# A hybrid HGRN2 and short-convolution layer on one core: tokens split from PSUM, their sums made in the first pairs, squares made later, small steps moved between engines

## The chip, the cores and the metric

The kernel runs on one core of one Trainium2 chip. The metric is the device time of one execution in microseconds. TensorE is PE in the rows below, VectorE is DVE, ScalarE is ACT, GpSimd is POOL, and SyncE is SP.

## The reference

One inference step of one decoder layer. The tokens are 16 meta tokens, a prompt of 512 and 8 samples of 4 tokens, 560 in all, 2048 wide. Cut to what matters:

```python
hn = rmsnorm(h, pre_norm_w)
proj = hn @ w_in                                  # 2048 -> 8192
q, fz, i, za, bg, cg, xt, zb = split(proj)        # 8 parts of 1024
f = lb + (1 - lb) * sigmoid(fz)                   # lb from softmax, cumsum
k = (1 - lb) * sigmoid(-fz);  v = i
o, S = hgrn(q, k, log(max(f, 1e-30)), v)          # S_t = f_t S_{t-1} + k_t v_t, o_t = S_t q_t; 8 heads of 128
o = rmsnorm(o, hgrn_norm_w) * silu(za)
c, new_buf = short_conv(cg * xt, buf, conv_w)     # causal, width 3
yb = bg * c * silu(zb)
h = h + rmsnorm(concat(o, yb) @ w_out, post_norm_w)
```

The outputs are the layer's result for prompt and samples, the new recurrent states and the new convolution buffers.

## The kernel before

**Input projection.** `w_in` is worked through in 32 *pairs* `p` of two blocks of 128 output columns, four pairs to each of 8 heads: 4i holds the forget gate and the input i, 4i+1 holds q and the gate za (the gate pair), 4i+2 holds C and x~ (the conv pair), 4i+3 holds B and zb. A pair has four raw blocks of 512 KB, named 11, 12, 21, 22 (which half of the output, which half of the 2048), loaded two pairs ahead by SP's queue into six buffers.

To multiply float32 in float16, a block is scaled by a power of two and split in a high and a low half: `split_w` makes the high on ScalarE (L290) and the low on VectorE (L291). The power comes from the sum of squares of the pair: `squares` (L263, ScalarE, with an accumulator) and `scale_of_weights` (L265 on), where a product with ones (`pss`, L275) sums over the partitions and `power` (L239 to L241) makes the scale. A product of two split operands is 24 matmuls: 8 chunks of 128 by three lines, L353 to L355 in `product`.

**Seven or eight products.** A plain pair takes eight block products. A pair for which `seven(p)` holds takes seven, with sums of weight blocks s1 to s4 (`sum_w`, L300, VectorE) and sums of token blocks t1 to t4 (`t_steps`, L454 on). Its plan is 11, s1, s2, 12, s3, s4, 22. Three partial results, m1, t and q, are put into SBUF by ScalarE (L370) so that their PSUM tile can be used again: product 3 writes where product 1 wrote, and the `sink` calls add them back on VectorE (L372, L374). `PLAIN` is the first pair that may take seven; before, it is 2.

**Tokens.** `turn_x(hf, k)` transposes 280 tokens by 128 features into PSUM. ScalarE copies that with the norm's weight to a float32 tile (`big`), POOL casts two of them to float16 (the high half), VectorE makes the low half. The token sums t1 to t4 are made from the float32 tiles during pair 1: two of them on POOL, two on VectorE.

**Order.** `pair(p)` runs the products of pair p; ahead of each, `step(j)` calls one of the next pair's preparations (`prep_steps(p + 1)`). Blocks 11 and 21 of pair p+2 are squared at step 5, the other two at the next pair's step 0. The recurrence of a head, the generator `attend`, is advanced in small pieces between the products of the pairs that follow; its tiles carry the names pd, vbd, lv, kc, pss, dm, ds, po, zur. In it, the intra-chunk part casts `vbd` on ScalarE (L688) for the products `lv` (L692); `dm` (L822) and `ds` (L827) form the state, in two PSUM banks that `pss` uses too; the rmsnorm of the head's output squares it (L842), sums (L849, L851), makes 1/sqrt by three Newton steps on VectorE (L858 to L860) and scales (L861). Up to the first lines of the recurrence the program keeps the written order; from there on a scheduler places the instructions by its own estimates, each engine then running its queue in order.

**After the projection** comes the output projection with the post norm (L973 on), which is not touched.

Of the kernel before, what the change touches and what calls it, by code (L numbers as in the profile page):

```python
# [64 lines left out]
def hymba_kernel(  # L65
# [389 lines left out]
    def t_steps():  # L455

        b11, b21, b12_, b22 = (bf[:, hf, KC * j:KC * j + KC] for hf in range(2) for j in range(2))

        def do(n, dst, a, b, op, eng, sign, c):
            c = slice(4 * c, 4 * c + 4)  # L460
            d = dst[:, c].rearrange("p k t -> p (k t)")
            h, l = (t[:, c].rearrange("p k t -> p (k t)") for t in xop(n))
            eng.tensor_tensor(d, a[:, c].rearrange("p k t -> p (k t)"), b[:, c].rearrange("p k t -> p (k t)"), op=op)
            A.activation(h, d, AF.Copy, scale=sign)
            V.scalar_tensor_tensor(l, d, sign, h, op0=ALU.mult, op1=ALU.subtract)

        for args in (("t1", b11, b11, b12_, ALU.subtract, G, 1.0), ("t3", b12_, b22, b12_, ALU.subtract, G, 1.0),
                     ("t2", b22, b22, b11, ALU.add, V, -1.0), ("t4", b21, b22, b21, ALU.subtract, V, 1.0)):
            for c in range(2):
                yield lambda args=args, c=c: do(*args, c)  # L470
# [191 lines left out]
    def attend(h, f, kb, q, vt, g):  # L662
# [185 lines left out]
        A.activation(sq[0:NS, SEQ:640], po_s, AF.Square)  # L848
        V.tensor_reduce(ssq[:, 0:4], sq[:, 0:SEQ].rearrange("p (j v) -> p j v", v=P),  # L849
                        axis=mybir.AxisListType.X, op=ALU.add)  # L850
        V.tensor_reduce(ssq[0:NS, 4:5], sq[0:NS, SEQ:640], axis=mybir.AxisListType.X, op=ALU.add)  # L851
# [9 lines left out]
        V.tensor_tensor(  # L861
            sq[:, 0:SEQ].rearrange("p (j v) -> p j v", v=P), po.rearrange("p (j v) -> p j v", v=P),
            r[:, 0:4].rearrange("p (j o) -> p j o", o=1).to_broadcast([P, 4, P]), op=ALU.mult,
        )
# [383 lines left out]
```

## Time and profile before

| | us |
|---|---|
| median of 3 runs | 1094.87 (1093.39 to 1099.02) |
| profiled execution, its own time | 1097.03 |
| its span on the core | 1095.3 |
| TensorE busy | 1015.4, 93% |
| VectorE busy | 819.2, 75% |
| ScalarE busy | 596.3, 54% |
| POOL busy | 77.5, 7% |

The mean granted clock of TensorE in the profiled execution is 0.972 of full speed. In the rows of groups by line and shape stands: line, engine, operation, output <- inputs with partitions x elements and type, count; then busy us and mean ns of one; then the idle time ahead of them and what ended it. In a timeline row: start, duration, engine, line, operation, and in brackets the idle time ahead with its releaser.

### The profile page before, as it was taken

What the parts mean: (1) busy time and instruction counts of PE and PEld (TensorE: products, weight loads), DVE (VectorE), ACT (ScalarE), POOL (GpSimd) and SP (SyncE); (2) the same over time, 40 slices, a digit from 0 to 9 for tenths busy, and PEclk for the clock granted to TensorE, in tenths of its full rate; (3) what the DMA queues carried; (4) which work ended last, traced back from release to release, by engine and by line L of the source; (5) the groups of instructions that cost most, each with busy time, mean ns of one, the idle gap of its engine ahead of it and who ended that gap; (6) DMA issues with size and microseconds to landing.
All of it is one profiled execution on the core that took longest, in us unless ns stands there. A gap on an engine that the chain in (4) does not pass through costs nothing.

```text
span 1095.3 us, 20032 instructions
## 1 busy us (share of the span) xinstructions
PE 1015.4 (93%) x8099; PEld 855.9 (78%) x8099; DVE 819.2 (75%) x1765; ACT 596.3 (54%) x1032; POOL 77.5 (7%) x83
## 2 busy tenths in 40 slices
PE   4798999989999999999999999999999999999995
PEld 3455878778777877787787778777778899999995
DVE  6468889888888988899889989888889762223226
ACT  4457846674566567466745665674566253232323
POOL 1362000000000000000000000000000010000004
PEclk9968999999999999999999999999999999999998
DMA  9212313441343224224503432242244154222104
GB/s 306 58 39 77 115 41 96 120 135 34 87 122 109 66 85 124 78 79 127 145 22 98 129 103 77 76 121 77 78 119 153 42 210 141 99 85 99 57 1 164
DMA packets 156931, 109.33 MB, mean 100 GB/s; under 512 B 3729, under 2 KB 151362, under 8 KB 155766
## 3 DMA queue, kind: packets, MB, share of 16 engines
q1 hardware_dynamic: 152934, 92.90, 28.6%
q0 software_dynamic: 3680, 14.49, 4.4%
q8 instruction: 63, 1.03, 0.4%
q10 hardware_dynamic: 224, 0.66, 0.2%
q14 instruction: 30, 0.25, 0.1%
HBM read 98.79 MB, written 9.25 MB: 99 GB/s over the span
## 4 chain that ended last, share of the span: by engine, by line
PE 36%; DVE 25%; DMA 18%; ACT 12%; issue 4%; POOL 1%; DVEq 0%; ACTq 0%; SPq 0%
DMA raw<-in_w_in_dram 18%; DVE ws L291 7%; DVE w L291 5%; ACT junk L263 4%; ACT w L290 4%; PE omm L1055 3%; PE omm L1056 3%; PE omm L1054 3%; DVE s L300 3%; PE omm L1064 2%; PE omm L1063 2%; PE omm L1062 2%; PE mm L353 2%; PE mm L354 2%; PE mm L355 2%
## 5 line engine op out<-in xcount | busy, mean ns | idle before, releaser
L263 ACT ACTIVATE junk<-raw 128x1024 uint8<-128x1024 f32 x120 | 126.8, 1057 | 131.8 <-DMA raw<-in_w_in_dram 130.9
L353 PE MATMUL mm<-x_b,w 128*128 128x272 f16 (+1 forms) x592 | 167.7, 283 | 0.9 <-ACT f L370 0.9
L354 PE MATMUL mm<-x_b,w 128*128 128x272 f16 (+1 forms) x592 | 167.3, 283 | 0.0
L355 PE MATMUL mm<-x_b,w 128*128 128x272 f16 (+1 forms) x592 | 167.2, 283 | 0.0
L291 DVE SCALAR_TENSOR_TENSOR w<-raw,sc,w 128x1024 f16<-128x1024 f32 x102 | 130.1, 1279 | 31.8 <-ACT w L290 30.9
L353 PEld LDWEIGHTS <-w 128*128 128x128 f16 x1120 | 110.5, 99 | 24.1 <-issue 1.4
L354 PEld LDWEIGHTS <-w 128*128 128x128 f16 x1120 | 110.5, 99 | 23.8 <-issue 2.9
L290 ACT ACTIVATE w<-raw,sc 128x1024 f16<-128x1024 f32 x102 | 115.7, 1139 | 22.9 <-DVE sc L241 18.9
L355 PEld LDWEIGHTS <-w 128*128 128x128 f16 x1120 | 110.5, 99 | 21.9
L353 PE MATMUL ma<-x_t,ws 128*128 128x274 f16 (+2 forms) x352 | 101.9, 290 | 17.1 <-ACT e L370 17.1
L354 PE MATMUL ma<-x_t,ws 128*128 128x274 f16 (+2 forms) x352 | 101.7, 289 | 0.0
L355 PE MATMUL ma<-x_t,ws 128*128 128x274 f16 (+2 forms) x352 | 101.7, 289 | 0.0
L185 DVE TENSOR_TENSOR wl<-rawo,wh 128x1024 fp32r<-128x1024 f32 x32 | 39.2, 1224 | 80.0 <-ACT wh L184 80.0
L290 ACT ACTIVATE ws<-s,sc 128x1024 f16<-128x1024 f32 x66 | 75.2, 1139 | 39.1 <-DVE s L300 37.9
L354 PEld LDWEIGHTS <-ws 128*128 128x128 f16 x704 | 70.2, 100 | 30.6 <-issue 17.1
L291 DVE SCALAR_TENSOR_TENSOR ws<-s,sc,ws 128x1024 f16<-128x1024 f32 x66 | 84.3, 1277 | 8.9 <-ACT ws L290 6.4
L353 PEld LDWEIGHTS <-ws 128*128 128x128 f16 x704 | 70.0, 99 | 16.6 <-issue 2.5
L355 PEld LDWEIGHTS <-ws 128*128 128x128 f16 x704 | 70.2, 100 | 15.2
L184 ACT CAST wh<-rawo 128x1024 fp32r<-128x1024 f32 x32 | 33.6, 1051 | 79.8 <-PE omm L1063 70.4
L1054 PE MATMUL omm<-mh,wh 128*128 128x288 f32 x256 | 75.8, 297 | 0.0
L1055 PE MATMUL omm<-ml,wh 128*128 128x288 f32 x256 | 75.6, 295 | 0.0
L1056 PE MATMUL omm<-mh,wl 128*128 128x288 f32 x256 | 75.4, 295 | 0.0
(317 smaller groups left out, 2671.9 us busy)
## 6 DMA issues: line engine op xcount, KB each, us to landing
raw<-in_w_in_dram SPq DMA_DIRECT2D x128, 512.0 KB, 4.2
rawo<-in_w_out_dram SPq DMA_DIRECT2D x32, 512.0 KB, 3.4
xp<-in_x_prompt_dram SPq DMA_DIRECT2D x4, 1024.0 KB, 10.6
s<-in_state_hgrn_dram POOLq DMA_DIRECT2D x8, 512.0 KB, 4.9
out_dram<-s POOLq DMA_DIRECT2D x8, 512.0 KB, 3.9
xres<-in_x_prompt_dram POOLq DMA_DIRECT2D x4, 1024.0 KB, 9.1
out_dram<-big SPq DMA_DIRECT2D x7, 256.0 KB, 2.8
wpo<-in_post_norm_w_dram POOLq DMA_DIRECT2D x4, 256.0 KB, 4.2
```

The source lines that it names most:

```text
L184: A.copy(wh, raw)
L185: V.tensor_tensor(wl, raw, wh.bitcast(F32), op=ALU.subtract)
L263: A.activation(junk, raws[p, key].rearrange("p k e -> p (k e)"), AF.Square, accum_out=t[:, c:c + 1])
L290: A.activation(w[:, 0], raw, AF.Copy, scale=s)
L291: V.scalar_tensor_tensor(w[:, 1].rearrange("p k e -> p (k e)"), raw.rearrange("p k e -> p (k e)"), s, w[:, 0].rearrange("p k e -> p (k e)" ...
L300: V.tensor_tensor(raws[p, key], raws[p, a], raws[p, b], op=ALU.add)
L353: T.matmul(o, w[:, 0, k, :], xh, start=first, stop=False, skip_group_check=onto)
L354: T.matmul(o, w[:, 0, k, :], xl, start=False, stop=False, skip_group_check=onto)
L355: T.matmul(o, w[:, 1, k, :], xh, start=False, stop=last, skip_group_check=onto)
L1054: T.matmul(o, wh[:, s_], mh[e][:, 0:SA], start=(e == 0), stop=False)
L1055: T.matmul(o, wh[:, s_], ml[e][:, 0:SA], start=False, stop=False)
L1056: T.matmul(o, wl[:, s_], mh[e][:, 0:SA], start=False, stop=(e == KT - 1))
```

## The change

- `PLAIN` goes from 2 to 5: pairs 2 and 4 take eight products, without weight sums.
- `turn_x`: ScalarE writes the high half straight from PSUM, VectorE the low half from PSUM; the float32 tiles and POOL's cast are gone. `sums_of_tokens` makes t1 to t4 from the split halves in four chunks of three steps, called in steps 1, 4 and 6 of the pairs from 1 on, all sums on VectorE.
- `squares`: all four blocks of pair p+1 in steps 0 and 1 of pair p; the first split follows at step 2, and s3 is made together with 12.
- `scale_of_weights`: the product with ones takes the four sums of squares as they are, in float32; the sum over the four comes behind it. Two small steps go to POOL.
- `attend` and its caller: the affine step of f goes to ScalarE, the copy of dm too; the squares of the head's output carry accumulators, which replace two reductions; the Newton steps go from 9 on VectorE to 12 on POOL; the scaling by the result goes to four ScalarE copies.

```diff
-PLAIN = 2
+PLAIN = 5
...
-        V.tensor_reduce(sc[:, 0:1], t[:, cols[0]:cols[1]], axis=AX.X, op=ALU.add)
-        V.tensor_copy(sb, sc[:, 0:1].to_broadcast([P, 2]))
...
-        T.matmul(ps[:, 0:2], ones_r, sb, start=True, stop=True)
-        power(sc[:, 0:1], ps[:, 0:1], MAGIC)
-        V.tensor_scalar(sc[:, 1:2].bitcast(I32), sc[:, 0:1].bitcast(I32), -1.0, sxk[:, 1:2], op0=ALU.mult, op1=ALU.add)
-        V.tensor_scalar(sc[:, 2:3], sc[:, 1:2], -1.0, None, op0=ALU.mult)
+        T.matmul(ps, ones_r.bitcast(F32), t[:, cols[0]:cols[1]], start=True, stop=True)
+        V.tensor_reduce(sc[:, 0:1], ps, axis=AX.X, op=ALU.add)
+        power(sc[:, 0:1], sc[:, 0:1], MAGIC)
+        G.tensor_scalar(sc[:, 1:2].bitcast(I32), sc[:, 0:1].bitcast(I32), -1.0, sxk[:, 1:2], op0=ALU.mult, op1=ALU.add)
+        G.tensor_scalar(sc[:, 2:3], sc[:, 1:2], -1.0, None, op0=ALU.mult)
...
     def prep_steps(p):
+        yield lambda: squares(p, ("11", "21"))
+        yield lambda: squares(p, ("22", "12"))
         if seven(p):
-            yield lambda: squares(p, ("22", "12"))
...
-            yield from (first, s1, s2, s3, lambda: split_w(p, "12"), last)
+            yield from (first, s1, s2, lambda: (split_w(p, "12"), s3()), last)
...
         def step(j):
-            if p == 1 and j == 0:
-                squares(2, ("11", "21"))
-            if seven(p) or j:
-                next(due, lambda: None)()
-            if j == 5 and p + 2 < NP:
-                squares(p + 2, ("11", "21"))
+            next(due, lambda: None)()
+            if j in (1, 4, 6):
+                next(t_steps, lambda: None)()
...
-        A.activation(bf[:, hf, k, :], ps[:, 24:24 + TH], AF.Copy, scale=wsc[:, k:k + 1])
-        if k % 2:
-            n = f"b{1 + k // KC}{1 + hf}"
-            kk = slice((k - 1) % KC, (k - 1) % KC + 2)
-            h, l = xop(n)
-            G.tensor_copy(h[:, kk], bf[:, hf, k - 1:k + 1])
-            V.tensor_tensor(l[:, kk], bf[:, hf, k - 1:k + 1], h[:, kk], op=ALU.subtract)
...
+        h, l = (t[:, k % KC] for t in xop(f"b{1 + k // KC}{1 + hf}"))
+        o, c = ps[:, 24:24 + TH], wsc[:, k:k + 1]
+        A.activation(h, o, AF.Copy, scale=c)
+        V.scalar_tensor_tensor(l, o, c, h, op0=ALU.mult, op1=ALU.subtract)
+
+    def sums_of_tokens():
+        for c in range(0, KC, 2):
...
+            def add(d, n, op, part=part):
+                for i in range(2):
+                    V.tensor_tensor(d, d, part(n, i), op=op)
+            def apart(d, a, b, part=part):
+                V.tensor_tensor(d, part(a, 0), part(b, 0), op=ALU.subtract)
+                V.tensor_tensor(d, d, part(a, 1), op=ALU.add)
+                V.tensor_tensor(d, d, part(b, 1), op=ALU.subtract)
+            def split(n, d, sign, part=part):
+                A.activation(part(n, 0), d, AF.Copy, scale=sign)
+                V.scalar_tensor_tensor(part(n, 1), d, sign, part(n, 0), op0=ALU.mult, op1=ALU.subtract)
+            yield lambda d=d, apart=apart, split=split: (apart(d, "b11", "b12"), split("t1", d, 1.0))
+            yield lambda d=d, add=add, split=split: (add(d, "b22", ALU.add), split("t2", d, -1.0),
+                                                     add(d, "b21", ALU.subtract), split("t4", d, 1.0))
+            yield lambda e=e, apart=apart, split=split: (apart(e, "b22", "b12"), split("t3", e, 1.0))
...
-        V.tensor_scalar(fu, fu, oml[:, h:h + 1], lb[:, h:h + 1], op0=ALU.mult, op1=ALU.add)
+        A.activation(fu, fu, AF.Identity, scale=oml[:, h:h + 1], bias=lb[:, h:h + 1])
...
-        V.tensor_copy(st[:, 0, :], dm[:, 0:P])
+        A.copy(st[:, 0, :], dm[:, 0:P])
...
-        A.activation(sq[:, 0:SEQ], po, AF.Square)
+        for j in range(4):
+            c = slice(j * P, (j + 1) * P)
+            A.activation(sq[:, c], po[:, c], AF.Square, accum_out=ssq[:, j:j + 1])
...
         for _ in range(3):
-            V.tensor_tensor(u, r, r, op=ALU.mult)
-            V.scalar_tensor_tensor(u, u, -0.5, z, op0=ALU.mult, op1=ALU.mult)
-            V.scalar_tensor_tensor(r, u, 1.5, r, op0=ALU.add, op1=ALU.mult)
...
+            G.tensor_tensor(u, r, r, op=ALU.mult)
+            G.tensor_tensor(u, u, z, op=ALU.mult)
+            G.tensor_scalar(u, u, -0.5, 1.5, op0=ALU.mult, op1=ALU.add)
+            G.tensor_tensor(r, r, u, op=ALU.mult)
+        for j in range(4):
+            c = slice(j * P, (j + 1) * P)
+            A.activation(sq[:, c], po[:, c], AF.Copy, scale=r[:, j:j + 1])
```

How the executed order moves, at three places. The first is ScalarE in the gate pair 13 of the fourth head, from the put of m1 (the first `e_13`) to that of q (the third). Before:

```order
L370 ACTIVATE e_13_4454<-ma_4451,sc_0_4189 128x272
L263 ACTIVATE junk,sq_4631<-raw_15_4445 128x1024
L290 ACTIVATE w_14_4495<-raw_14_4131,sc_0_4485 128x1024
L290 ACTIVATE ws_14_4525<-s_14_4523,sc_0_4485 128x1024
L370 ACTIVATE e_13_4456<-mc_4452,sc_0_4189 128x272
L290 ACTIVATE ws_14_4561<-s_14_4523,sc_0_4485 128x1024
L370 ACTIVATE e_13_4455<-ma_4451,sc_0_4189 128x272
```

And now, from the f steps on:

```order
L655 ACTIVATE f<-f,par 128x560
L263 ACTIVATE junk,sq_4765<-raw_15_4489 128x1024
L368 ACTIVATE e_13_4500<-ma_4497,sc_0_4270 128x272
L263 ACTIVATE junk,sq_4765<-raw_15_4491 128x1024
L368 ACTIVATE e_13_4502<-mc_4498,sc_0_4270 128x272
L288 ACTIVATE w_14_4567<-raw_14_4172,sc_0_4558 128x1024
L288 ACTIVATE ws_14_4604<-s_14_4602,sc_0_4558 128x1024
L368 ACTIVATE e_13_4501<-ma_4497,sc_0_4270 128x272
L288 ACTIVATE ws_14_4640<-s_14_4602,sc_0_4558 128x1024
```

The put of q now stands ahead of the second `ws_14` of s1 and s2; the put of m1 now stands behind the affine step of f (L655) and one of pair 15's squares.

The second is ScalarE in the conv pair 14 around the cast of `vbd` (squares are the rows of `junk`). Before:

```order
L290 ACTIVATE w_15_4906<-raw_15_4447,sc_0_4749 128x1024
L263 ACTIVATE junk,sq_4909<-raw_16_4711 128x1024
L263 ACTIVATE junk,sq_4909<-raw_16_4713 128x1024
L263 ACTIVATE junk,sq_5232<-raw_17_5015 128x1024
L688 CAST vbd<-pd 128x256
L760 COPY kc<-kb 128x256
```

And now:

```order
L288 ACTIVATE w_15_4948<-raw_15_4491,sc_0_4829 128x1024
L288 ACTIVATE w_15_4995<-raw_15_4493,sc_0_4829 128x1024
L263 ACTIVATE junk,sq_5066<-raw_16_4755 128x1024
L686 CAST vbd<-pd 128x256
L263 ACTIVATE junk,sq_5066<-raw_16_4757 128x1024
L758 COPY kc<-kb 128x256
L263 ACTIVATE junk,sq_5400<-raw_17_5057 128x1024
L263 ACTIVATE junk,sq_5400<-raw_17_5059 128x1024
```

The cast has two squares of the next pairs less ahead of it.

The third is TensorE in pair 16, the first of the fifth head, where the scale product `pss` of pair 17 and the state's `dm` and `ds` stand. Before, the scale product came between the first product and mc, and 12 matmuls of mc later dm and ds:

```order
L355 MATMUL ma_5354<-x_b_79,w_16_5101 128x280
L275 MATMUL pss_0_5407<-sb_0_5403,ones_r 128x2
L353 LDWEIGHTS ws_16_5151
L353 MATMUL mc_5355<-x_t_83,ws_16_5151 128x280
L354 LDWEIGHTS ws_16_5151
L354 MATMUL mc_5355<-x_t_83,ws_16_5151 128x280
```

Now dm and ds stand at that place of mc and the scale product comes 12 matmuls later, behind mc:

```order
L353 LDWEIGHTS ws_16_5194
L353 MATMUL mc_5395<-x_t_83,ws_16_5194 128x280
L820 MATMUL dm<-big,ktm 128x128
L825 MATMUL ds<-v,kt 128x128 x4
L351 LDWEIGHTS ws_16_5194
L351 MATMUL mc_5395<-x_t_83,ws_16_5194 128x280
```

So dm and ds no longer follow the scale product in the banks they share.

## Rows read from the trace of the kernel before

**Rows 1.** The page: busy time by engine; TensorE's clock in 40 slices.

```profile
PE 1015.4 (93%) x8099; PEld 855.9 (78%) x8099; DVE 819.2 (75%) x1765; ACT 596.3 (54%) x1032; POOL 77.5 (7%) x83
...
PEclk9968999999999999999999999999999999999998
```

**Rows 2.** TensorE's waits, whole span: us in total, times, longest.

```profile
PE ma L353 <- ACT e L370: 17.1, 8, 2.7
PE lv L692 <- ACT vbd L688: 11.9, 6, 2.9
...
PE ds L827 <- DVE sc L239: 7.4, 7, 1.2
PE mm L61 <- POOL x_b L61: 5.1, 1, 5.1
PE pss L61 <- DVE sb L61: 3.8, 3, 2.2
...
PE pss L275 <- DVE sb L272: 2.3, 1, 2.3
PE mm L61 <- DVE x_b L61: 2.1, 4, 0.8
```

**Rows 3.** Windows: us; busy (count) PE, PEld, DVE, ACT, POOL; PEclk; DMA share; GB/s.

```profile
65.50:75.00 9.50, 9.50 (x37) 5.35 (x36) 7.57 (x8) 5.86 (x12) 6.22 (x4) 0.50 0.19 57
84.00:98.00 14.00, 10.88 (x61) 7.37 (x60) 13.35 (x17) 10.10 (x20) 5.13 (x6) 0.70 0.00 0
109.00:112.50 3.50, 3.50 (x19) 2.40 (x17) 3.32 (x8) 3.48 (x4) 0.00 (x0) 0.55 0.00 0
822.70:826.00 3.30, 3.30 (x18) 2.20 (x16) 3.30 (x8) 2.21 (x4) 0.00 (x0) 0.50 0.26 77
```

**Rows 4.** Groups by line and shape on VectorE, whole span.

```profile
L300 DVE TENSOR_TENSOR s<-s,raw 128x1024 f32<-128x1024 f32 x44 | 53.6, 1218 | 0.8
...
L61 DVE TENSOR_TENSOR x_b<-big,x_b 128x560 f16<-128x560 f32 x16 | 22.4, 1408 | 18.5 <-POOL x_b L61 18.5
...
L465 DVE SCALAR_TENSOR_TENSOR x_t<-big,x_t 128x1120 f16<-128x1120 f32 x8 | 10.5, 1316 | 0.0
...
L953 DVE SCALAR_TENSOR_TENSOR y<-mm,sc,y 128x272 f32<-128x272 f32 x16 | 7.9, 493 | 9.3 <-PE pss L275 6.4 <-PE mm L355 2.9
...
L463 DVE TENSOR_TENSOR big<-big 128x1120 f32<-128x1120 f32 x4 | 5.3, 1320 | 0.1
...
L860 DVE SCALAR_TENSOR_TENSOR zur<-zur 128x5 f32<-128x5 f32 x24 | 3.9, 161 | 0.6
```

**Rows 5.** Timeline of TensorE: a scale product; two products of a gate pair begin.

```profile
91.38 0.24 PE L61 MATMUL pss<-sb,ones_r 128*128 128x2 f32 x1 [2.19 <-DVE sb L61]
...
408.80 0.29 PE L353 MATMUL mc<-x_t,ws 128*128 128x272 f16 x1
...
411.59 0.28 PE L353 MATMUL ma<-x_t,ws 128*128 128x272 f16 x1
```

**Rows 6.** Timeline of POOL around 416 us.

```profile
416.08 0.89 POOL L664 DMA_DIRECT2D s<-in_state_hgrn_dram  x1 [4.46 <-ACT e L370]
```

**Rows 7.** Groups by line and shape on ScalarE, whole span.

```profile
L263 ACT ACTIVATE junk<-raw 128x1024 uint8<-128x1024 f32 x120 | 126.8, 1057 | 131.8 <-DMA raw<-in_w_in_dram 130.9
...
L263 ACT ACTIVATION_READ_ACCUMULATOR junk<-raw 128x1 f32 x120 | 22.5, 188 | 0.0
...
L656 ACT ACTIVATE f<-f 128x560 f32<-128x560 f32 x8 | 5.4, 669 | 0.2
...
L370 ACT ACTIVATE vt<-ma,sc 128x128 f32<-128x128 f32 x14 | 4.3, 363 | 0.0
```

**Rows 8.** Timeline of ScalarE: the m1 put of a gate pair.

```profile
409.57 0.49 ACT L370 ACTIVATE e<-ma,sc 128x272 f32<-128x272 f32 x1
```

**Rows 9.** Groups by line and shape on POOL, whole span.

```profile
L463 POOL TENSOR_TENSOR big<-big 128x1120 f32<-128x1120 f32 x4 | 11.7, 2918 | 0.0
...
L61 POOL COPY turned<-ident 48x8 f32<-48x8 f32 x3 | 0.5, 183 | 0.1
```

More of the change, by code (lines that the diff above doesn't have):

```diff
@@ L268, in scale_of_weights @@
         t = sws[p]
-        sb = wpool.tile([P, 2], F32R, name=f"sb_{p}_{cols[0]}", tag="sb", bufs=1)
         sc = wpool.tile([P, 3], F32, name=f"sc_{p}_{cols[0]}", tag="sc", bufs=3)
-        V.tensor_reduce(sc[:, 0:1], t[:, cols[0]:cols[1]], axis=AX.X, op=ALU.add)
-        V.tensor_copy(sb, sc[:, 0:1].to_broadcast([P, 2]))
         pool = {"tr": ps_tr, "lv": ps_lv}[tag]
-        ps = pool.tile([P, SEQ], F32, name=f"pss_{p}_{cols[0]}", tag=tag)
-        T.matmul(ps[:, 0:2], ones_r, sb, start=True, stop=True)
-        power(sc[:, 0:1], ps[:, 0:1], MAGIC)
-        V.tensor_scalar(sc[:, 1:2].bitcast(I32), sc[:, 0:1].bitcast(I32), -1.0, sxk[:, 1:2], op0=ALU.mult, op1=ALU.add)
-        V.tensor_scalar(sc[:, 2:3], sc[:, 1:2], -1.0, None, op0=ALU.mult)
+        ps = pool.tile([P, SEQ], F32, name=f"pss_{p}_{cols[0]}", tag=tag)[:, 0:cols[1] - cols[0]]
+        T.matmul(ps, ones_r.bitcast(F32), t[:, cols[0]:cols[1]], start=True, stop=True)
[3 more added lines that the diff above has]
+        G.tensor_scalar(sc[:, 2:3], sc[:, 1:2], -1.0, None, op0=ALU.mult)
         return sc
@@ L326, in last @@
                 split_w(p, "22")
-            yield from (first, s1, s2, s3, lambda: split_w(p, "12"), last)
+            yield from (first, s1, s2, lambda: (split_w(p, "12"), s3()), last)
             return
-        yield lambda: squares(p, ("22", "12"))
         yield lambda: scs.__setitem__(p, [scale_of_weights(p)] * 2)
@@ L374, in put, with pair @@
             V.scalar_tensor_tensor(dst, o, c[:, 2:3], add, op0=ALU.mult, op1=ALU.subtract)
-    def pair(p, off, sink, extra=()):
+    def pair(p, off, sink):
         n = TH - off
@@ L381, in pair @@
         due = iter(nxt)
-        extra = iter(extra)
         def step(j):
-            if p == 1 and j == 0:
-                squares(2, ("11", "21"))
-            if seven(p) or j:
-                next(due, lambda: None)()
-            if j == 5 and p + 2 < NP:
-                squares(p + 2, ("11", "21"))
+            next(due, lambda: None)()
+            if j in (1, 4, 6):
+                next(t_steps, lambda: None)()
         if not seven(p):
@@ L397, in pair @@
                 step(j)
-                next(extra, lambda: None)()
                 product(o, p, f"{i + 1}{kk + 1}", f"b{kk + 1}{hf + 1}", off, kk == 0, kk == 1)
@@ L446, in turn_x @@
             T.transpose(ps[:, 48 + b * P:48 + (b + 1) * P], xp[2 * hf + b][:, ks], ident)
-        A.activation(bf[:, hf, k, :], ps[:, 24:24 + TH], AF.Copy, scale=wsc[:, k:k + 1])
-        if k % 2:
-            n = f"b{1 + k // KC}{1 + hf}"
-            kk = slice((k - 1) % KC, (k - 1) % KC + 2)
-            h, l = xop(n)
-            G.tensor_copy(h[:, kk], bf[:, hf, k - 1:k + 1])
-            V.tensor_tensor(l[:, kk], bf[:, hf, k - 1:k + 1], h[:, kk], op=ALU.subtract)
[L455 to L470, printed above, removed]
@@ new lines, in turn_x, with part @@
+        h, l = (t[:, k % KC] for t in xop(f"b{1 + k // KC}{1 + hf}"))
[4 more added lines that the diff above has]
+        for c in range(0, KC, 2):
+            def part(n, i, c=c):
+                return xo[n][:, i, c:c + 2].rearrange("p k t -> p (k t)")
+            d, e = (flat[:, a * NOUT:a * NOUT + 2 * TH] for a in (6, 14))
+            def add(d, n, op, part=part):
[12 more added lines that the diff above has]
+            yield lambda e=e, apart=apart, split=split: (apart(e, "b22", "b12"), split("t3", e, 1.0))
@@ L472, in hymba_kernel @@
+    t_steps = sums_of_tokens()
     scale_of_tokens()
@@ L530, in hymba_kernel @@
             turn_x(1, k)
-        if k == 8:
-            squares(1, ("11", "21"))
-        if k in (12, 16):
+        if k in (8, 12, 16):
             next(steps1)()
@@ L650, in qz @@
                 V.tensor_tensor(two(g)[:, hf], two(g)[:, hf], zs, op=ALU.mult)
-        pair(p0 + 1, 8, qz, t_steps() if first else ())
+        pair(p0 + 1, 8, qz)
         kb = tl("kb", 640)
@@ L847, in attend @@
         T.matmul(po_s, fold, sel, start=False, stop=True)
[L848 to L851, printed above, removed]
+        A.activation(sq[0:NS, SEQ:640], po_s, AF.Square, accum_out=ssq[0:NS, 4:5])
         zur = tl("zur", 15)
@@ L857, in attend @@
         for _ in range(3):
-            V.tensor_tensor(u, r, r, op=ALU.mult)
-            V.scalar_tensor_tensor(u, u, -0.5, z, op0=ALU.mult, op1=ALU.mult)
-            V.scalar_tensor_tensor(r, u, 1.5, r, op0=ALU.add, op1=ALU.mult)
[L861 to L864, printed above, removed]
+            G.tensor_tensor(u, r, r, op=ALU.mult)
[5 more added lines that the diff above has]
+            A.activation(sq[:, c], po[:, c], AF.Copy, scale=r[:, j:j + 1])
         V.tensor_scalar(sq[0:NS, SEQ:640], po_s, r[0:NS, 4:5], None, op0=ALU.mult)
```

## The prediction

> **What bounds the kernel now.** I read the page's engine shares first, then the waits of TensorE, then the windows, and only then the rows of single operations. TensorE is busy for 93% of the span and VectorE for 75% [rows 1]. So the time is TensorE's work plus its waits plus what the clock takes. The list of TensorE's waits [rows 2] shows few causes. Three come back in every head: the s3 product of a gate pair waits for the q put by ScalarE (17.1 us in 8), the lv products of a conv pair for ScalarE's vbd cast (11.9 in 6), and ds for VectorE reading a pss bank (7.4 in 7). The others stand before the first full pair: 5.1 and 2.1 for the token tiles, 3.8 and 2.3 for the sb that feeds pss. Almost everywhere the granted clock is at full speed [rows 1]. The windows [rows 3] give the second price of a wait: from 109.0 to 112.5 us it is 0.55, and from 822.7 to 826.0 it is 0.50, half speed, 1.2 in place of 2.4 GHz. Seven such stretches, these being the first and the last, stand behind waits; they are about 3.1 us long, so each loses some 1.55 us. I measure my sum against the profiled execution, 1097.0 us, which stands 2.2 above the median of the runs.
>
> **The change, part by part.**
>
> 1. *Token tiles straight from PSUM.* The POOL cast and VectorE's subtract of 128x560 leave; per k VectorE now reads the PSUM tile once. The nearest row is a 272-column one from PSUM, 0.493 us [rows 4], so 32 x 0.49 = 15.8 in place of 22.4 us, and POOL is out of the chain. TensorE's waits for x_b go: 5.1 + 2.1 = **-7.2**. Ends: 0 (VectorE, now also carrying the first token sums here, is late instead) and -7.2.
>
> 2. *Scale chain.* The pss product reads the sums of squares themselves, so two VectorE steps before it go, and VectorE's queue is no longer in front of it: 3.8 + 2.3 = **-6.1**, with 0 as the other end if ScalarE's squares are late instead. The 61 products of the stretch from 84 to 98 us cost 10.9 us at clock 0.70 [rows 3]; at full clock they are 7.1, at 2.79 us for 24 [rows 5]. I take half of that, **-1.9**. The pss product itself becomes plain float32, 30 of them; the row of today's is 0.24 us [rows 5], and a few hundredths more each make **+1**. The two last steps go to POOL, behind its DMA issues: the state load at 416.08 us waited 4.46 before it was issued [rows 6]. Their first reader is the first put of the conv pair, 7 products of 2.79 us behind 408.80 [rows 5], thus 428.3, so they cost nothing while that issue is less than 11 us late.
>
> 3. *Two plain pairs more.* Eight products in place of seven in pairs 2 and 4: 2 x 2.79 = **+5.6** [rows 5]. There is nothing to hide it behind.
>
> 4. *Token sums on VectorE.* Forty sums of 128x560 at 0.66 and 16 splits at 0.66 (halves of the 1.320 and 1.316 rows) are 37 us, a quarter of it in the turning stage. Against that 15.8 us leave (4 sums, 8 splits of 1120), and pairs 2 and 4 drop 4 sums of 1.22 and 3 splits of about that each, 8.5 us a pair [rows 4]. Up to pair 3 VectorE has 28 - 15.8 - 8.5 = 3.7 us more to do. It was busy for 13.35 of the 14 us from 84 to 98 [rows 3], so I take it to be late by all of that, **+4**; ends 0 and +9, the latter if pair 2's relief comes too late.
>
> 5. *ds behind pss.* In the first pair of a head the scale product now stands behind ds, and the dm copy is ScalarE's, so VectorE's reading of pss holds nothing up: 7.4 less 0.4 left = **-7**; ends 0 and -7.4.
>
> 6. *vbd in the conv pair.* The cast stands ahead of two of the squares that wait for a load. Idle time before squares is 131.8 us over 120, 1.1 each, and a square takes 1.057 + 0.188 [rows 7]. Two in front fewer are 4.7 us, and the waits were up to 2.9 long. I leave 0.2 a head: **-10.5**; ends 0 and -11.9.
>
> 7. *The puts in the gate pair.* q is now put ahead of the second split, so the wait of 17.1 us goes. But ahead of the m1 put, which the third product needs, ScalarE now also does four scaled copies (0.363 each), the f affine (0.67) and a whole square (1.25): 3.4 us [rows 7]. The put ended at 409.57 + 0.49 [rows 8] and was needed at 411.59 [rows 5]: 1.5 us of slack. Newton's steps come from POOL: 12 x 0.2 (part 9) in place of 9 x 0.16 [rows 4], 1.0 later, one wait for a load (1.1) leaves, and TensorE itself arrives some 0.5 earlier. So 3.4 + 1.0 + 0.5 - 1.5 - 1.1 = 2.3 us a head, 16 in 7, a new wait for almost the same price: **-1**. Ends: -17 (none comes) and +16 (twice as long).
>
> 8. *The clock.* Four of the seven half-speed stretches follow waits that I let go: 4 x 1.55 = **-6.2** [rows 3]. Ends 0 and -10.9.
>
> 9. *Newton on POOL.* VectorE sheds nine steps of 0.16 and the reductions; off the path, except through the queues: ScalarE's copies wait for r (counted in 7), and VectorE's scaling of the sample rows stands waiting for r ahead of the f evacuation. No POOL row has this shape. Bounds: 0.183 us (the copy of 48x8) and 2.92 (two inputs, 128x1120) [rows 9]; I take 0.2, since 5 columns are nearest to the small copy. At that POOL's 2.4 us stand against the 1.45 us of steps and the reductions that VectorE sheds: **0**.
>
> Sum: -7.2 - 6.1 - 1.9 + 1 + 5.6 + 4 - 7 - 10.5 - 1 - 6.2 = -29.3. From 1097.0 that is 1067.7; against the median, 2.2 lower, 1065.6, thus **1066**.
>
> A float32 sum of two inputs took 2918 ns on POOL and 1320 on VectorE for the same 128x1120, 2.2 times as long [rows 4, 9]. The Trainium skill speaks against the move: GPSIMD Engine Reference, section 3, Performance versus the Vector engine, puts two-input elementwise work at about twice VectorE's time and advises leaving it there. The trace agrees on the large tile; no run here shows a tile of 5 columns. By that rule a step would be an estimated 0.32 us, 1.4 us a head later than I took, and the sum would come to about 1076.
>
> **The rivals.**
>
> *All waits go.* ScalarE has 54% load [rows 1]; if it keeps ahead, m1 is in time, and part 7 is worth -17: 1066 - 16 = 1050. If the clock also holds through the second turning, which ran at 0.50 from 65.5 us on for some 18 us [rows 3], up to 9 us more come back; 6 of them give 1044. For it: the waits were of 2 to 3 us, about one square with its load. Against: 3.4 us are put ahead of m1, and the slack was 1.5. Chance 0.20.
>
> *It does not do all it says: squares hardly move in the executed order.* The order is a scheduler's; in the conv pair two squares move only behind the cast, by two or three rows, and the last one ahead of it waits for a load as before. Then part 6 gives nothing: 1066 + 10.5 = 1076. For it: nearly all the idle time ahead of squares, 130.9 of 131.8 us, is put down to loads, which the change does not touch [rows 7]. Against: the order has the cast ahead of two of them. Chance 0.15.
>
> *Waits change place.* Parts 5 to 8 give nothing, since ScalarE and VectorE are in-order and another wait takes the place of each: -7.2 - 6.1 - 1.9 + 1 + 5.6 + 4 = -4.6, 1090. For it: VectorE is at 75% on the whole and about 95% in the early stretch. Against: the three waits have three different causes, all named in the diff. Chance 0.13.
>
> *Slower: Newton on POOL.* Per head, 12 steps of t, with ScalarE's copies and VectorE's queue, and so the f evacuation and m1, behind them. Each 0.1 us on t is 1.2 us a head, 8.4 in 7. The gain is gone from t = 0.2 + 29.3/84 = 0.55; at t = 0.7 it is 42 - 29 = 13 slower, 1108. For it: POOL's 2.2 times on the large tile, and hand-overs between engines at both ends. At 2.2 times VectorE's 0.161 a step would be 0.35 and the time 1079, still faster; to be slower it needs more than that. Against: POOL's copy of 48x8 at 0.183. Chance 0.10.
>
> **How the numbers follow.** The forecast has 0.42, the rivals 0.20, 0.15, 0.13 and 0.10. The forecast, the first and the second rival are faster by over 0.5% (5.5 us, about what a measurement of this kernel can tell from no change): 0.77; the third is within it but for a little on either side, the last slower but for a little: **0.78, 0.12, 0.10**. The range leaves out the fastest end (all waits gone and the clock held, below 1044) and the slower rival: **1044 to 1091**.
>
> **What would show it.** Right: no TensorE wait for POOL x_b or DVE sb; the ds and vbd entries near nothing; a wait for the ScalarE put that now stands at the third product of gate pairs, about 2 us; about four half-speed stretches fewer; POOL's steps on zur at about 0.2 us each; 48 more matmuls at the lines of the product. Wrong: vbd waits of 2 us a head (part 6), m1 in time (part 7), POOL steps above 0.5, or TensorE waiting for a split in pairs 1 to 4 because VectorE is behind (part 4).

## The result, and the profile after

The changed kernel takes 1059.2 us (median of 4 runs, 1058.34 to 1069.3) against 1094.9 for the kernel before: a ratio of 0.9689, with an interval of 0.9625 to 0.9753. That is 35.7 us less; 28.9 were forecast, with a range of 1044 to 1091. The total came out; where it came from did not, as the rows show.

The page of the changed kernel, engine shares and clock in 40 slices:

```profile
PE 1002.9 (95%) x8180; PEld 854.4 (81%) x8180; DVE 775.0 (73%) x1588; ACT 608.0 (57%) x1152; POOL 97.4 (9%) x225
...
PEclk9999999999999999999999999999999999999998
```

TensorE has 81 more records, as 24 more matmuls for each of two products and the split pss products bring, and is busy for less time [rows 1]. Its waits, us in total, times, longest:

```profile
PE ma L351 <- ACT e L368: 13.2, 11, 1.9
...
PE pss L272 <- ACT st L821: 1.9, 5, 0.6
PE pss L272 <- ACT junk L263: 1.8, 1, 1.8
PE mm L61 <- DVE x_b L61: 1.7, 2, 0.9
PE xt L61 <- DVE x_b L61: 1.6, 2, 1.0
...
PE lv L690 <- ACT vbd L686: 0.8, 2, 0.6
```

Against [rows 2]: the vbd wait fell from 11.9 to 0.8, the wait of ds for VectorE's sc is gone, POOL x_b and DVE sb are gone. The wait for a put kept most of its size, 17.1 before and 13.2 now, and changed its place; six of its 11 entries are of 1.9 us and make up 11.4. It is the one of the third product, which needs m1's tile:

```profile
378.49 0.28 PE L351 MATMUL ma<-x_t,ws 128*128 128x272 f16 x1 [1.88 <-ACT e L368]
```

To see where the time went I set three marks in both traces: the last transpose group of the second turning, and the `dm` products (one a head) of the second and seventh head.

| stretch | before, us | after, us | difference |
|---|---|---|---|
| start to the last turning step | 82.4 | 56.7 | -25.7 |
| to dm of head 2 (holds the two more products, +5.6) | 201.2 | 194.3 | -6.9 |
| dm of head 2 to dm of head 7, five heads | 501.7 | 494.1 | -7.6 |
| to the output projection | 100.3 | 101.0 | +0.7 |
| output projection, to the end | 209.6 | 211.4 | +1.8 |

Two thirds of the gain lie in the opening, up to the last turning step, in which the two kernels do nearly the same work on TensorE. TensorE's waits there fell from 23.6 to 16.2 us, 7.4 of the 25.7; the rest is the same work done faster. The timeline shows how: a step of the second turning (three transposes, three matmuls) took 1.59 us before,

```profile
65.64 0.34 PE L61 MATMUL xt<-turned,xs 48*128 48x48 f32 x1
65.91 0.69 PE L61 MATMUL xt<-ident,xp 128*128 128x128 f32 x2
66.39 0.90 PE L61 MATMUL mm<-x_b,w 128*128 128x280 f16 x3
67.23 0.34 PE L61 MATMUL xt<-turned,xs 48*128 48x48 f32 x1
```

and takes 0.91 now,

```profile
52.12 0.26 PE L61 MATMUL xt<-turned,xs 48*128 48x48 f32 x1
52.31 0.44 PE L61 MATMUL xt<-ident,xp 128*128 128x128 f32 x2
52.58 0.52 PE L61 MATMUL mm<-x_b,w 128*128 128x280 f16 x3
53.03 0.26 PE L61 MATMUL xt<-turned,xs 48*128 48x48 f32 x1
```

The windows give the clock with it: 0.50 from 65.5 to 75 us before [rows 3], and now, over nearly all of the second turning (columns as in [rows 3]):

```profile
47.00:57.00 10.00, 10.00 (x71) 6.75 (x71) 7.62 (x21) 9.16 (x20) 0.00 (x0) 1.00 0.19 54
```

The first turning went from 1.6 to 0.9 us a step, by the same durations.

### The profile page after: what moved, and what is told of

It is laid out like the page before. It is cut to its first block, busy times and chain, and to the rows that moved or that the text cites. A ratio compares the mean times of both kernels' runs of the same rounds, so it can differ in the third digit from the quotient of the medians.

```text
span 1057.5 us, 20349 instructions
## 1 busy us (share of the span) xinstructions
PE 1002.9 (95%) x8180; PEld 854.4 (81%) x8180; DVE 775.0 (73%) x1588; ACT 608.0 (57%) x1152; POOL 97.4 (9%) x225
## 4 chain that ended last, share of the span: by engine, by line
PE 39%; DVE 25%; DMA 15%; ACT 13%; issue 5%; POOL 2%; SPq 0%; DVEq 0%; ACTq 0%; POOLq 0%
DMA raw<-in_w_in_dram 15%; DVE w L289 6%; ACT w L288 4%; DVE ws L289 4%; ACT junk L263 4%; PE omm L1052 3%; PE omm L1053 3%; PE omm L1051 3%; PE omm L1060 3%; PE omm L1061 3%; PE omm L1059 3%; DVE s L298 2%; PE ma L351 2%; PE ma L353 2%; PE ma L352 2%
## 5 line engine op out<-in xcount | busy, mean ns | idle before, releaser
L351 PE MATMUL mm<-x_b,w 128*128 128x272 f16 (+2 forms) x720 | 202.3, 281 | 0.0
L353 PE MATMUL mm<-x_b,w 128*128 128x272 f16 (+2 forms) x720 | 202.0, 281 | 0.0
L352 PE MATMUL mm<-x_b,w 128*128 128x272 f16 (+2 forms) x720 | 202.0, 281 | 0.0
L351 PEld LDWEIGHTS <-w 128*128 128x128 f16 x1200 | 118.5, 99 | 25.1 <-issue 1.8
L352 PEld LDWEIGHTS <-w 128*128 128x128 f16 x1200 | 117.7, 98 | 25.5 <-issue 4.0
L288 ACT ACTIVATE w<-raw,sc 128x1024 f16<-128x1024 f32 x104 | 116.2, 1140 | 35.7 <-DVE sc L241 35.6
L353 PEld LDWEIGHTS <-w 128*128 128x128 f16 x1200 | 117.7, 98 | 22.8
L351 PE MATMUL ma<-x_t,ws 128*128 128x272 f16 (+2 forms) x320 | 91.8, 287 | 13.4 <-ACT e L368 13.2
L288 ACT ACTIVATE ws<-s,sc 128x1024 f16<-128x1024 f32 x60 | 68.7, 1145 | 57.5 <-DVE s L298 47.2
L353 PE MATMUL ma<-x_t,ws 128*128 128x272 f16 (+2 forms) x320 | 91.8, 287 | 0.0
L352 PE MATMUL ma<-x_t,ws 128*128 128x272 f16 (+2 forms) x320 | 91.6, 286 | 0.0
L352 PEld LDWEIGHTS <-ws 128*128 128x128 f16 x640 | 63.3, 99 | 26.6 <-issue 14.8
L289 DVE SCALAR_TENSOR_TENSOR ws<-s,sc,ws 128x1024 f16<-128x1024 f32 x60 | 76.5, 1275 | 9.6 <-ACT ws L288 9.6
L351 PEld LDWEIGHTS <-ws 128*128 128x128 f16 x640 | 64.8, 101 | 14.4 <-issue 2.2
L353 PEld LDWEIGHTS <-ws 128*128 128x128 f16 x640 | 63.2, 99 | 13.1
```

Of the source, the lines that this page charges most:

```text
L288: A.activation(w[:, 0], raw, AF.Copy, scale=s)
L289: V.scalar_tensor_tensor(w[:, 1].rearrange("p k e -> p (k e)"), raw.rearrange("p k e -> p (k e)"), s, w[:, 0].rearrange("p k e -> p (k e)" ...
L351: T.matmul(o, w[:, 0, k, :], xh, start=first, stop=False, skip_group_check=onto)
L352: T.matmul(o, w[:, 0, k, :], xl, start=False, stop=False, skip_group_check=onto)
L353: T.matmul(o, w[:, 1, k, :], xh, start=False, stop=last, skip_group_check=onto)
```

## The experiments

Each kernel is one edit away from a version named with it; k and l join three. The ratio is to the kernel before, run beside it. *Head* is the mean of the five distances from dm to dm (second to seventh head); the steps are of the first and second turning, late in each. Both are read from the one profiled execution of each kernel. Kernels with the same code in the heads differ in them: before and d by 0.6 us, and after, c, h and i lie between 98.22 and 98.81, so a smaller difference in *head* shows nothing.

| run | us | ratio, interval | head, us | steps, us |
|---|---|---|---|---|
| before | 1094.9 | | 100.35 | 1.6, 1.6 |
| after | 1059.2 | 0.9689 (0.9625 to 0.9753) | 98.81 | 0.9, 0.9 |
| a_scale_old | 1069.2 | 0.9770 (0.9724 to 0.9817) | 98.77 | 1.6, 0.9 |
| b_scale_new | 1093.8 | 1.0006 (0.9983 to 1.0028) | 101.73 | 1.6, 1.6 |
| c_turn_old | 1082.1 | 0.9889 (0.9848 to 0.9931) | 98.42 | 1.6, 1.6 |
| d_tokens_new | 1088.7 | 0.9953 (0.9927 to 0.9980) | 101.00 | 1.6, 0.9 |
| e_newton_dve | 1053.6 | 0.9635 (0.9598 to 0.9673) | 98.37 | 0.9, 0.9 |
| f_head_old | 1059.8 | 0.9683 (0.9633 to 0.9733) | 98.10 | 1.6, 0.9 |
| g_squares_old | 1088.1 | 0.9951 (0.9917 to 0.9986) | 103.82 | 1.6, 0.9 |
| h_plain4 | 1055.2 | 0.9667 (0.9612 to 0.9723) | 98.22 | 0.9, 0.9 |
| s_squares_new | 1078.1 | 0.9841 (0.9818 to 0.9864) | 98.61 | 1.6, 1.6 |
| i_warm8 | 1059.0 | 0.9666 (0.9643 to 0.9688) | 98.64 | 0.9, 0.9 |
| k_best_newton | 1054.9 | 0.9633 (0.9610 to 0.9656) | 98.35 | 0.9, 0.9 |
| l_best_head | 1055.9 | 0.9638 (0.9617 to 0.9658) | 97.93 | 0.9, 0.9 |

**What sets the clock of the turnings.** Two edits undo a part in the changed kernel, two put a part alone into the kernel before.

a_scale_old, in `scale_of_weights` of the changed kernel:

```diff
+        V.tensor_reduce(sc[:, 0:1], t[:, cols[0]:cols[1]], axis=AX.X, op=ALU.add)
+        V.tensor_copy(sb, sc[:, 0:1].to_broadcast([P, 2]))
-        T.matmul(ps, ones_r.bitcast(F32), t[:, cols[0]:cols[1]], start=True, stop=True)
-        V.tensor_reduce(sc[:, 0:1], ps, axis=AX.X, op=ALU.add)
+        T.matmul(ps[:, 0:2], ones_r, sb, start=True, stop=True)
```

> The changed kernel with only the old head of the scale chain (VectorE reduce and cast to sb, pss in the replicated-float form). If the wait of pss for VectorE's sb in the warm-up (0.74 us at 18 us in the kernel before) is what kept the clock down, both turnings run at half speed again, a step of the first turning takes 1.58 us in place of 0.92, and the time is about 1059 + 20 = 1079. If the way of the tokens through POOL kept it down, the turnings stay at 0.92 a step and only the waits for sb come back, 4 to 6 us: about 1064.

b_scale_new is the reverse of this in the kernel before.

> The kernel before with only the new head of the scale chain. If the warm-up's wait kept the clock down, the first turning runs at 0.92 us a step and the time falls by some 15 to 25: about 1075. If POOL's way kept it down, the steps stay at 1.58 and only the waits for sb go: about 1089.

c_turn_old, in `turn_x` of the changed kernel:

```diff
-        A.activation(h, o, AF.Copy, scale=c)
-        V.scalar_tensor_tensor(l, o, c, h, op0=ALU.mult, op1=ALU.subtract)
+        A.activation(bf[:, hf, k, :], ps[:, 24:24 + TH], AF.Copy, scale=wsc[:, k:k + 1])
+        if k % 2:
...
+            G.tensor_copy(h[:, kk], bf[:, hf, k - 1:k + 1])
+            V.tensor_tensor(l[:, kk], bf[:, hf, k - 1:k + 1], h[:, kk], op=ALU.subtract)
```

> The changed kernel with the old way of the token tiles (float32 copy, POOL cast, VectorE subtract), sums still made from the halves. If POOL's way kept the clock down, the turnings are at 1.58 us a step again, with waits for x_b of 5 to 7: about 1059 + 27 = 1086. If the warm-up's wait kept it down, the steps stay at 0.92 and only waits for x_b come back: about 1065.

d_tokens_new puts the new `turn_x`, `sums_of_tokens`, its calls and `PLAIN = 5` into the kernel before.

> The kernel before with only the token part: tiles straight from PSUM, sums in pairs 1 to 4 on VectorE, PLAIN 5; scale chain, squares and the head's small steps as before. If POOL's way is the cause, the turnings run at 0.92 us a step and most of the gain is here: about 1070. If the warm-up's wait is, they stay at 1.58 and the time is about 1095 - 7 + 6 = 1094.

Neither theory was right alone. The second turning follows the tokens' way in all of these: 0.9 us a step with tiles straight from PSUM (a, d), 1.6 with POOL in between (b, c). The first turning was fast to its end only where both parts were in, though both did not always suffice (f and g, below). In a it is slow from its first step, behind a pss that waited for sb (timeline of TensorE, a_scale_old):

```profile
15.59 2.08 PE L61 MATMUL warm<-ident,raw 128*128 128x128 f32 x8 [10.24 <-DMA raw<-in_w_in_dram]
18.55 0.37 PE L61 MATMUL pss<-sb,ones_r 128*128 128x2 f32 x1 [0.88 <-DVE sb L61]
...
22.51 0.34 PE L61 MATMUL xt<-turned,xs 48*128 48x48 f32 x1
22.78 0.69 PE L61 MATMUL xt<-ident,xp 128*128 128x128 f32 x2
```

In c it begins fast and is slow behind the wait for POOL (c_turn_old):

```profile
25.93 0.26 PE L61 MATMUL xt<-turned,xs 48*128 48x48 f32 x1 [0.81 <-ACT big L61]
26.12 0.44 PE L61 MATMUL xt<-ident,xp 128*128 128x128 f32 x2
32.67 0.39 PE L61 MATMUL mm<-x_b,w 128*128 128x280 f16 x1 [6.12 <-POOL x_b L61]
33.86 0.63 PE L61 MATMUL mm<-x_b,w 128*128 128x280 f16 x2 [0.80 <-DVE x_b L61]
34.41 0.34 PE L61 MATMUL xt<-turned,xs 48*128 48x48 f32 x1
34.69 0.69 PE L61 MATMUL xt<-ident,xp 128*128 128x128 f32 x2
```

So in b the first turning gains little: what it wins at its start, the wait for POOL takes away, and the whole opening is 4.6 us shorter than before. That b as a whole brings nothing has another reason: its trace is 12.3 us ahead at dm of head 2 and loses 6.9 of it in the next five heads (101.73 each), in which five half-speed stretches stand where before has three. Why it has more of them is open. The token part is worth 22.9 us inside the change (c against after) and 4.7 alone (d). In d's trace it saved 11.4 us up to dm of head 2, but its heads took 101.0. The speed of the first turning in the other executions of these kernels is not on record: a's four times run from 1064.3 to 1073.0, the profiled one being the longest, and one of d's ten is 1079.7, the others 1086.6 and more.

**The heads.** In the changed kernel one part each is undone.

e_newton_dve:

```diff
-            G.tensor_tensor(u, r, r, op=ALU.mult)
-            G.tensor_tensor(u, u, z, op=ALU.mult)
-            G.tensor_scalar(u, u, -0.5, 1.5, op0=ALU.mult, op1=ALU.add)
-            G.tensor_tensor(r, r, u, op=ALU.mult)
+            V.tensor_tensor(u, r, r, op=ALU.mult)
+            V.scalar_tensor_tensor(u, u, -0.5, z, op0=ALU.mult, op1=ALU.mult)
+            V.scalar_tensor_tensor(r, u, 1.5, r, op0=ALU.add, op1=ALU.mult)
```

> The changed kernel with the nine Newton steps back on VectorE, nothing else. In the changed kernel POOL takes 3.3 us from the first of its 12 steps to the last, and TensorE then waits 1.9 us for the put of m1 at the third product of gate pairs. If POOL's chain is what makes that put late, the steps take about 1.6 us, the wait goes almost wholly and the time falls by about 8, to 1051. If ScalarE's own work ahead of the put (copies, f affine, a square) makes it late, the wait stays above 1 us a head and the time stays within 3 of 1059.

f_head_old goes further; the copy of dm, the f affine, the reductions and the scaling are as before too:

```diff
-        A.activation(fu, fu, AF.Identity, scale=oml[:, h:h + 1], bias=lb[:, h:h + 1])
+        V.tensor_scalar(fu, fu, oml[:, h:h + 1], lb[:, h:h + 1], op0=ALU.mult, op1=ALU.add)
...
-        A.copy(st[:, 0, :], dm[:, 0:P])
+        V.tensor_copy(st[:, 0, :], dm[:, 0:P])
```

> The changed kernel with all small steps of the head as before: f affine, dm copy, reductions, Newton and scaling on VectorE. If ScalarE's work ahead of m1 together with POOL's chain makes the wait, it goes: about 1049. If the moves took load from VectorE that was needed, VectorE is late in its stead, and with the waits for ds back (7) the time is 1062 or more.

g_squares_old, in the step of `pair` (and in `prep_steps` and the second turning accordingly):

```diff
-            next(due, lambda: None)()
+            if p == 1 and j == 0:
+                squares(2, ("11", "21"))
+            if seven(p) or j:
+                next(due, lambda: None)()
+            if j == 5 and p + 2 < NP:
+                squares(p + 2, ("11", "21"))
```

> The changed kernel with the squares where they were (two blocks of pair p+2 at step 5, two at the next pair's step 0) and s3 ahead of 12. If the shift of the squares is what freed the vbd cast, the wait of lv for vbd comes back, about 1.7 a head, and the time is about 1059 + 10 = 1069. If the other moves freed it, the time stays within 3 of 1059.

h_plain4:

```diff
-PLAIN = 5
+PLAIN = 4
...
-            if j in (1, 4, 6):
+            if j in (1, 3, 5, 6):
```

> The changed kernel with PLAIN 4 and the token sums called four times a pair, so that all are done in pairs 1 to 3 and pair 4 takes seven products again. If VectorE has room in pairs 1 to 3 this saves one product, 2.8 us: about 1056. If it has none, TensorE waits for splits there and the time is 1059 or more.

s_squares_new is the reverse of g in the kernel before.

> The kernel before with only the shift of the squares (all four blocks of pair p+1 in steps 0 and 1 of pair p, s3 made with 12). If the shift alone is the gain of the heads, the wait of lv for vbd goes, a head takes 98 us in place of 100.3 and the time is about 1093 - 15 = 1078; the turnings stay at 1.58 us a step. If it needs the small steps too, a head stays above 100 and the time within 5 of 1093.

**With Newton back on VectorE the time is 5.6 us less, but the order moved too** (e against after, 1053.6 to 1059.2). All four times of e, up to 1055.5, lie below all four of after, from 1058.3; the intervals of the two ratios overlap. The chain that ended last, in the changed kernel, runs through POOL's steps (start, us, what):

```profile
367.17 0.20 POOL zur L855
367.38 0.07 issue
367.45 0.20 POOL zur L856
...
370.24 0.21 POOL zur L858
370.44 0.02 issue
370.47 0.03 ACT sq L861
```

A step took 0.20 us, but 0.07 lay between any two, so the twelve took 3.3 us. VectorE stood for the result too (its groups by line: busy, mean ns, idle ahead):

```profile
L862 DVE TENSOR_SCALAR sq<-pso,zur 32x128 f32<-32x128 f32 x8 | 2.7, 339 | 19.1 <-POOL zur L858 19.1
```

Yet this is not what makes the put of m1 late. ScalarE's timeline around that put, in the gate pair 13, in the changed kernel:

```profile
375.50 0.79 ACT L657 ACTIVATE kb<-kb,par 128x560 f32<-128x560 f32 x1
376.15 0.87 ACT L655 ACTIVATE f<-f,par 128x560 f32<-128x560 f32 x1
376.90 1.07 ACT L263 ACTIVATE junk<-raw 128x1024 uint8<-128x1024 f32 x1
...
377.94 0.50 ACT L368 ACTIVATE e<-ma,sc 128x272 f32<-128x272 f32 x1
```

and in e_newton_dve:

```profile
375.34 0.79 ACT L657 ACTIVATE kb<-kb,par 128x560 f32<-128x560 f32 x1
375.99 0.51 ACT L368 ACTIVATE e<-ma,sc 128x272 f32<-128x272 f32 x1
376.36 0.88 ACT L655 ACTIVATE f<-f,par 128x560 f32<-128x560 f32 x1
377.11 1.08 ACT L263 ACTIVATE junk<-raw 128x1024 uint8<-128x1024 f32 x1
```

ScalarE reaches the step of kb at the same time in both. In the changed kernel the affine step of f and a square then stand ahead of the put, in e behind it, and the put starts 1.95 us earlier. So it is in each of the six heads that have the wait; the step of kb starts 26.2 us behind the dm before it in the changed kernel and 26.4 in e, on average. The wait of 1.9 us is the price of these two, as the second theory of the expectation had it; its forecast, that the wait stays, failed because the scheduler, given other steps for Newton, put m1 ahead of them.

The waits as a whole hardly fell: from dm of head 1 to the output projection TensorE's are 21.4 us in the changed kernel and 20.4 in e, where smaller ones came (waits of e_newton_dve):

```profile
PE ma L351 <- ACT e L368: 7.3, 16, 1.2
PE ma L351 <- DVE g L372: 5.7, 7, 0.9
```

What went with the long waits is half speed. Three of the six waits of 1.9 us are followed within about 1 us by a half-speed stretch, this one behind the wait at 378.49; the other three are not:

```profile
378.90:382.30 3.40, 3.40 (x17) 2.34 (x16) 2.01 (x8) 3.14 (x5) 1.93 (x2) 0.52 0.16 19
```

The three are 8.3 us long at a granted clock of 0.50 to 0.52 and so cost some 4.1; in e no head has one. With the 1.0 us of waits that is about what lies between the two traces, 4.3 us over the same stretch. What POOL's slower chain costs by itself is not isolated: k below, which is h with Newton on VectorE, e's order and a longer warm-up, takes 1054.9 against h's 1055.2, so no gain is left there.

**The shift of the squares is the gain of the heads.** Alone in the kernel before it saves 17 us (ratio 0.9841), as its theory had it: no vbd entry is left among TensorE's waits, and none of ds for VectorE's sc either, and the head falls from 100.35 to 98.61, though the put's wait stands at 21.0. Of the 20.3 us between the two traces 9.4 lie ahead of dm of head 2 and 8.7 in the next five heads. Its waits:

```profile
PE ma L353 <- ACT e L370: 21.0, 13, 2.4
...
PE mm L61 <- POOL x_b L61: 6.1, 1, 6.1
```

Undone in the changed kernel it costs 28.9, far more than the 10 expected. The profiled execution of g, at 1096.2 the longest of ten (the shortest 1081.0), is 36.6 us longer than that of after. Some 8 of these lie in the opening, with the first turning at half speed (below). The heads take 5.0 us more each: the vbd wait and the ds wait are back, and VectorE is late for the next products (g_squares_old). VectorE stands for POOL's r for 23.1 us in 8 there, against 19.1 in after; that this makes it late is not shown. TensorE's waits in g:

```profile
PE ma L351 <- DVE g L372: 12.1, 7, 2.6
PE lv L697 <- ACT vbd L693: 10.9, 6, 3.0
...
PE ma L351 <- DVE vt L372: 9.4, 6, 1.7
PE ds L832 <- DVE sc L273: 6.3, 6, 1.1
```

With the old squares the new scale chain alone makes a head slower (b, 101.73 against 100.35), and with the small steps moved too it is 103.82; with the new squares the old small steps are 0.7 faster than the new (98.10 in f), hardly more than such heads differ by. So no gain of the small steps shows in the heads. The ds wait settles the same way: it is gone in s, and in f with dm's copy on VectorE, and is there in g with the copy on ScalarE (6.3 us). In s, f and after the scale product stands some 3 us behind dm in these heads, in g, as before, 1.6 us ahead of it. So the wait follows the place of the squares, and with it of the scale product, and not the copy of dm.

**The first turning in f and g.** Both have the early code of the changed kernel, and both ran the first turning slow in the profiled execution; the times of f were 1052.7, 1057.4 and twice 1062.3, those of after once 1069.3. In f ScalarE's square was 0.2 us late for pss (f_head_old):

```profile
17.32 0.58 PE L61 MATMUL pss<-sq,ones_r 128*128 128x2 f32 x2 [0.21 <-ACT junk L61]
...
21.49 0.34 PE L61 MATMUL xt<-turned,xs 48*128 48x48 f32 x1
```

That asked for a warm-up that cannot run out, i_warm8 in the changed kernel:

```diff
-    keep_busy(4, raws[0, "12"][:, 0, :])
+    keep_busy(8, raws[0, "12"][:, 0, :])
```

> The changed kernel with eight in place of four warm-up products ahead of the first scale product, so that TensorE has no pause while ScalarE squares the second block. If the pause ahead of that product decides whether the first turning runs at full speed, every execution has it at 0.92 us a step, and the times lie within 3 us of 1059 with none near 1069. If it is decided elsewhere, some executions stay some 9 us longer.

The turning began at full speed, and the five times lay between 1056.5 and 1059.8 (timeline, i_warm8):

```profile
14.79 3.78 PE L61 MATMUL warm<-ident,raw 128*128 128x128 f32 x16 [9.46 <-DMA raw<-in_w_in_dram]
18.37 0.42 PE L61 MATMUL pss<-sq,ones_r 128*128 128x2 f32 x2
...
21.82 0.26 PE L61 MATMUL xt<-turned,xs 48*128 48x48 f32 x1
22.01 0.44 PE L61 MATMUL xt<-ident,xp 128*128 128x128 f32 x2
```

Of the three kernels with eight (this one and the two below) the profiled executions have both turnings at full speed, and each kernel's times, 13 in all, lie within 3.9 us of each other. What decides it with four is not settled: in s the turning rose to full speed behind a pss that had waited 0.48 us, and in g it did not though no wait is recorded.

**Putting it together.** k_best_newton is e, h and i in one; l_best_head is f, h and i in one.

> Newton on VectorE, PLAIN 4 with the token sums in pairs 1 to 3, and eight warm-up products. If the three gains add up: 1059 - 6 - 4 = 1049. If Newton's place and the sums press on VectorE together, 1053 or more.

> All the head's small steps as in the kernel before, PLAIN 4 with the token sums in pairs 1 to 3, and eight warm-up products. f_head_old took 1052.7 in its fastest execution and 1062.3 in two others, in the profiled one with the first turning at half speed. If that is the warm-up's doing, the times now lie close together, about 1049; if the small steps matter, 1053 or more, and if VectorE is too full for sums and small steps together, 1058.

Both have a lower median than the changed kernel, at 0.9633 and 0.9638, with intervals that reach into its own, and neither beats e (0.9635). The gains do not add up: in k TensorE's waits for VectorE's vt and g come to 4.1 and 5.4.

## Why the prediction was right, and where it was not

The sign, the range and the total held, the total by luck: the opening gave far more than the sum had, and the heads far less.

- **Parts 1 and 2, tokens and scale chain.** Of the waits of 13.3 us those for POOL and for sb went as written; 1.7 of the 2.1 for VectorE's x_b stayed, and 1.6 and 1.8 of others came (waits of after). What failed is the clock's place in them: the step took 1.9 us for it in the stretch from 84 to 98 and left "the clock holds through the second turning" to a rival at 0.20. Both turnings went to full speed: from first to last step 28.5 to 14.3 us and 21.5 to 13.1. The rows at hand showed 0.50 from 65.5 us on; whether the waits that were to go caused it, I did not ask.
- **Part 3, two more products:** +5.6 stands in the count. h_plain4 took one of them back and measured 4.0 less, with intervals that overlap; at dm of head 2 its trace is 2.2 us ahead.
- **Part 4, token sums:** the +4 did not come. TensorE's waits in pairs 1 to 4 have none for a split, and h puts the sums in three pairs with no loss that shows.
- **Parts 5 and 6, ds and vbd:** right in the waits. The ds wait went, with 1.9 of pss for ScalarE's st in its place; vbd went to 0.8 for 1.4 left. g and s show that the squares did both; part 5 also named ScalarE's copy of dm, which f and g show to be no part of it. The rival in which squares hardly move is ruled out by s.
- **Part 7, the m1 put:** right in place and nearly in size: 13.2 us in 11 for 16 in 7, 1.9 for six heads where 2.3 was worked out. Of its terms, the affine step of f and the square ahead of the put bear it out, 1.8 us by the timelines above; the 1.0 for Newton's later end does not show, since ScalarE reaches the step ahead of them as late in e.
- **Part 8, clock in the heads:** four stretches fewer of seven were expected. Counting by the spacing of the product's matmuls, the kernel before has these seven and two more between 84 and 98 us; after has four, one in the early pairs and three behind the new m1 wait.
- **Part 9, Newton.** 0.2 us a step was right (means of 195 to 231 ns by line). The 0.07 between steps was left out, and that VectorE stands while POOL works (19.1 us in 8) was named and priced at 0. The sum had put 7 us for the move, inside part 7; e gave 5.6 by its medians, by its trace through the order and the clock, and k against h gave 0.3. So the price is open, and the rival in which a step of over 0.55 makes the kernel slower is ruled out. The Trainium skill's rule (GPSIMD Engine Reference, section 3, about twice VectorE's time) is not what the trace shows for 128x5: 195 to 231 ns here against 159 to 161 on VectorE before, 1.2 to 1.4 times. That no gain of the move shows agrees with its steer away from POOL.
- **How the two errors met.** Up to dm of head 2 the sum had -4.6 (parts 1 to 4 with the clock of part 2) and one of seven heads' share of parts 5 to 8, 3.5: -8.1; measured -32.6. From there on it had -21.2; measured -5.1. For the five heads to dm of head 7 it had -17.6, and -7.6 came: the waits fell by 10.9 where 13.2 were put down for five heads, the half-speed stretches there went from three to two, some 1.5 for 4.4, and the scale products in two passes gave some 2 back (0.26 us from the matmul ahead of one to the matmul behind it, where it was 0.15; 3.2 over all 30, where +1 was put down). Some 3 us of the difference stay open. The total came out because the opening gave more than the sum had, and the heads less.

## What to carry to other kernels

A wait in a short opening stage can cost several times its length when TensorE runs the stage at half speed, as here: compare the duration of one repeated step across stages before pricing the wait. Look which work stands ahead of a cast or put in an in-order queue and move it as a whole (here the squares, 17 us alone), before moving small steps between engines. And where a scheduler places the instructions, read the executed order of an experiment too: taking back one small step moved a put ahead of two others, and the wait that went with it was theirs.

## What the runs showed that I had not expected

- The granted clock of the windows does not show everything: the first turning of the kernel before has durations of half speed (0.34, 0.69, 0.90, as in the second) and the windows give 1.00 for it:

```profile
36.40:51.10 14.70, 13.85 (x53) 7.85 (x53) 6.51 (x14) 6.84 (x12) 2.62 (x4) 1.00 0.24 73
```

- By its durations the first turning ran at either speed in kernels with the same opening (after and f: 14.3 and 21.2 us from first to last step), and the times of one kernel spread by as much (f by 9.7 us and after by 11.0); with four more warm-up products no such spread is left in 13 executions.
- The output projection, which no edit touches, took 209.6 to 209.7 us in the profiles of before, a, d and s, and 211.3 to 211.5 in all others. The first four are the kernels with the old scale chain, the others those with the new one. Why that matters behind the projection is open.
